# A pad of 48 or 64 floats ahead of the stationary tiles, and when a fourth weight buffer is given up

## The chip, the core and the metric

The kernel runs on one core of a Trainium2 chip. The metric is device time in microseconds, the median of several runs. TensorE (PE) multiplies: it loads a stationary 128 x 128 tile (PEld) and streams a moving one of up to 512 columns past it into PSUM. ScalarE (ACT) and VectorE (DVE) work on tiles in SBUF and PSUM, GpSimd (POOL) mostly issues a few DMAs, and SyncE (SP) issues the DMAs that load the weights. SBUF has 128 partitions; a tile's address is its byte offset within each partition.

## The reference, cut to what matters

Two layers on 256 tokens of width 2048, all in float32. Layer 0 mixes tokens with a convolution module, layer 1 with latent attention of 16 heads. Behind each mixer stands an MLP of width 8192:

```python
for layer in range(DEPTH):
    h = rms_norm(x, norm_mixer_g[layer])
    x = x + (conv_module(h, ...) if layer % 2 == 0 else mla(h, ...))
    h = rms_norm(x, norm_mlp_g[layer])
    x = x + jnp.square(jax.nn.relu(h @ mlp_w1[layer])) @ mlp_w2[layer]
return rms_norm(x, final_norm_g)
```

The MLPs hold most of the arithmetic: x @ w1 (2048 to 8192) and its square's product with w2 (8192 to 2048), twice.

## The kernel before

**Split operands.** A float32 operand is split into an upper part (`hi`, rounded to the matmul's format, made by ScalarE, L465 or L180) and the rest (`lo` = value - `hi`, by VectorE, L466 or L184). A product is then three matmuls, stationary high x moving high, stationary low x moving high, stationary high x moving low (`mm3`, L213 to L215), each with up to 512 columns. Weights arrive by DMA in a `raw` buffer of 1 MB (8 KB in each partition), are split into `hi` and `lo` tiles (six each), and both are moving operands here.

**The MLP.** The hidden width is worked in two halves (`half`, hf = 0 and 1). A half first makes 8 groups g of 512 hidden columns. Each group takes four up units of 1 MB of w1 (`up_products`, L811 and L812; here the weights are stationary and the activations `xt` move), then its four PSUM banks are squared and split into stationary tiles `gh`/`gl`, `mh`/`ml`, `sh`/`sl`, or `dh`/`dl` for the last group (`forms`). Which name a group has depends on how many of its two blocks are worked by Strassen's scheme: none (g = 3 and 6: gh), one (g = 5: mh) or both (g = 0, 1, 2, 4: sh), while g = 7 has a place of its own (dh). Then come two down passes, n = 0 and n = 2, each over 1024 of the 2048 output columns and each of 16 units: 7 plain units (`PlainQuad`, 1 MB of w2, 24 matmuls) and 9 mixed units (`MixedQuad`, Strassen's seven products, 21 matmuls, three DMAs, and sums by VectorE at L516, L520, L521 between its splits). So a half has 32 up units (28 in a first half, whose first group stands ahead) and 32 down units.

**The order.** `run` goes through the list `units` and emits, for each unit i: loads of later units into whatever raw buffers are free (in order of the units), the second split of unit i, the first split of unit i + 1, the further sums and splits of unit i if it is mixed (and then also the second split of a plain unit i + 1, ahead of unit i's last split), the unit's matmuls, and then what hangs in `u.after`. Each engine keeps this order. SP issues loads in this order too, and a load at the head of its queue that waits for its buffer holds back what is behind it.

**The fourth buffer.** There are three raw buffers. At the end of a half's up units the last quarter of `xt` (tag "last", row blocks 12 to 15 of the activations, 8 KB in each partition) is not needed any more, and `open_down` makes it a fourth raw buffer. In a first half it is needed again by the next half's up units: `xt` was copied to DRAM (`save`, L887), and `fetch` (L890) loads it back in pieces of two row blocks. So `retire_raw` gives the fourth buffer up behind unit 11 of pass n = 2, after which no unit is loaded into it, and behind unit 15, the last one, `open_last` makes it the last quarter of `xt` again and `fetch` loads row blocks 12 and 13, 14 and 15. The next half's up units with u = 3 read them. In a second half there is no fetch.

**Places in SBUF.** Pools are stacked from the left: constants, `main` (the residual `xs`), `wpool` (raw, hi, lo), `small`, and behind it the pool of the stage at work: the convolution's, the MLP's (`mp`) or the attention's. A second stack grows from the right: `xt` and what stands in its place (`dh`, `dl` and four `room` tiles beside the fourth raw buffer). Tiles named `pad_...` only take up room. `pad_small`, of `PAD_SMALL` floats in each partition, is the first tile of `small`, so its size moves all tiles of the stages' left pools, and none of wpool or of the right stack.

Of the kernel before, what the change touches and what calls it, by code (L numbers as in the profile page):

```python
# [35 lines left out]
CHUNK = 64  # L36
HALVES = 2
PAD_CONST = 8
PAD_SMALL = 48
PAD_RIGHT = 48  # L40
PAD_KV = 8
PAD_O = 56
# [38 lines left out]
def trunk_kernel(  # L81
# [50 lines left out]
    for i, eps in enumerate((EPS, LN_EPS)):  # L132
        eps_cols[eps] = pad_const[:, i : i + 1]
        nc.vector.memset(eps_cols[eps], eps)
    small.tile([P, PAD_SMALL], F32, tag="pad_small", name="pad_small", bufs=1)
    edge = ctx.enter_context(tc.tile_pool(name="edge", bufs=1, side="right"))
# [238 lines left out]
    def open_rest(name):  # L375
        xt[2] = xt_tile(right_pool(name, 1, 1), KC // 2, "rest")

    def xrows(k, n):
        i, at = ((0, 0), (2, 4), (2, 4), (3, 12))[k // 4]
        return xt[i][:, k - at : k - at + n, :]  # L380
# [174 lines left out]
    class Sums:  # L555
# [19 lines left out]
        def mixed(self, b, fh, fl, end):  # L575

            self.open(True)
            u1, u6, u7, u5 = self.u
            work = [
                (self.e[0][1], 5, b.b22), (u5, 6, b.q1), (u1, 0, b.b11), (self.e[0][0], 1, b.b21),  # L580
                (u6, 3, b.q2), (u7, 4, b.q3), (self.e[1][0], 2, b.q4),
            ]
            for ps, i, (wh, wl) in work:
                mm3(ps, fh[:, i, :], fl[:, i, :], wh, wl, self.first(ps), end and any(ps is u for u in self.u))
# [109 lines left out]
    def mlp(layer, ssq, next_gain, finish=None, before=None, between=None, beside=None, after_up=None):  # L694

        with ExitStack() as cx:
# [16 lines left out]
            ks = [4 * g + 2 * b for g, b in plain]  # L713
            mixed = lambda g: [b for b in range(2) if (g, b) in ms]
            number = [sum(len(mixed(g)) == n for g in range(ng)) for n in range(3)]
            units, rstd = [], []

            def raw_tile():
                return wpool.tile([P, 4 * NB], F32, tag="raw", name=nm("raw"), bufs=3)
# [23 lines left out]
            def run():  # L743


                todo = list(units)
                for i, u in enumerate(units):
                    while todo and any(e not in held for e in free):
                        e, e.place = todo.pop(0), [p for p in free if p not in held][0]
                        free.remove(e.place)  # L750
                        e.load(e.place())
                    if i == 0:
                        u.first()
                        u.main_sum()
                    u.second()
                    for e in units[i - 1].mid if i else ():
                        e()
                    for e in u.at:
                        e()
                    ahead = units[i + 1 : i + 2]  # L760
                    for e in ahead:
                        e.first()
                    u.other_sums()
                    for e in ahead:
                        e.main_sum()
                    u.third()
                    if isinstance(u, MixedQuad):
                        for e in ahead:
                            if not isinstance(e, MixedQuad):
                                e.second()  # L770
                    u.fourth()
                    free.append(u.place)
                    u.products(u)
                    for e in u.after:
                        e()

            def scales():
# [87 lines left out]
            def half(hf):  # L865
# [23 lines left out]
                def fetch(k):  # L889
                    nc.sync.dma_start(xrows(k, 2).bitcast(F32), spare[:, k : k + 2, :])  # L890
# [45 lines left out]
                def mixed_unit(sums, i):  # L936
                    g, b = ms[i]

                    def src():
                        top, low = row_of((sums.n, i))  # L940
                        return top[:, :NB], low, made[sums.n, i]

                    unit(MixedQuad, src, lambda q: sums.mixed(q, *gs[g][b], i == len(ms) - 1))

                def plain_unit(sums, k, at=(), end=False):
                    unit(
                        PlainQuad, rows(w, k_lo + k, 2, sums.n * NB, 2 * NB),
                        lambda q: sums.plain(q.parts, hi, lo, k, end), at,
                    )

                for n in range(0, NNB, 2):
                    sums = Sums(n, (0, 1) if n == 0 else () if last else (1,))
                    final = last and n == NNB - 2
                    order = ks if n == 0 else ks[-2:] + ks[:-2]
                    head = HEAD[n // 2]
                    tail = LAST_TAIL if final and finish is not None else 2 if final else 1
                    inner = len(order) - head - tail
                    m, start = 0, len(units)
                    for i, k in enumerate(order[: len(order) - tail]):
                        plain_unit(sums, k)  # L960
                        if i < head - 1:
                            continue
                        upto = -(-len(ms) * (i - head + 2) // (inner + 1))
                        while m < upto:
                            mixed_unit(sums, m)
                            m += 1
                    if final:
                        for i in range(2):
                            units[-4 + i].after.append(lambda i=i: prepare(i, what="s"))
                        break  # L970
                    plain_unit(sums, order[-1], [lambda sums=sums: sums.join(room)], True)
                    closing.append([lambda sums=sums, n=n: sums.close(down_room if n == 0 else room)])
                    if n:
                        units[start + 4].after.append(lambda: open_rest(f"xt{layer}{hf}"))
                        for i, k in enumerate(range(KC // 4, 3 * KC // 4, 2)):
                            units[start + 5 + 2 * i].after.append(lambda k=k: fetch(k))
                        units[start + 11].after.append(retire_raw)
                        units[start + 15].after.append(open_last)
                        for k in (12, 14):
                            units[start + 15].after.append(lambda k=k: fetch(k))  # L980
                if not last:
                    return

                with tc.manual_schedule():
                    run()
# [27 lines left out]
            for hf in range(HALVES):  # L1013
                nssq = half(hf)
# [4 lines left out]
    with ExitStack() as cx:  # L1019
# [235 lines left out]
        with tc.manual_schedule():  # L1255
# [272 lines left out]
            for m in range(NP):  # L1528
# [4 lines left out]
                for j in range(2):  # L1533
                    k = 2 * m + j
# [19 lines left out]
                for q in {NP - 3: (0, 1, 4), NP - 2: (5, 2, 3), NP - 1: (6, 7)}.get(m, ()):  # L1554
                    t, i = divmod(q, NNB)
# [13 lines left out]
    def rotary_tables():  # L1569
# [60 lines left out]
        nc.scalar.activation(cos, an2, AF.Sin)  # L1630

    ssq = mlp(0, ssq, g_mix[1], beside=rotary_tables)
    repool("a", acc=6, tr=2)


    with ExitStack() as cx:
# [23 lines left out]
        units, pieces = [], {}  # L1660
# [184 lines left out]
        later = []  # L1845
# [112 lines left out]
        with tc.manual_schedule():  # L1958
# [9 lines left out]
            for k in range(KC):  # L1968
                u, j = divmod(k, 2)
# [17 lines left out]
            for k in range(KC):  # L1987
                u, j = divmod(k, 4)
# [105 lines left out]
    with ExitStack():  # L2094
# [60 lines left out]
        def between(ssq, t):  # L2155
# [5 lines left out]
            gained(t, n)  # L2161

        mlp(1, ssq, None, finish, before, between, after_up=load_gf)


# [24 lines left out]
```

## Time and profile before

| What | Value |
|---|---|
| Median of 3 runs (lowest, highest) | 1941.53 us (1941.08, 1941.58) |
| The profiled execution, its own time | 1941.04 us |
| Its span in the profile | 1939.3 us |
| Granted TensorE clock, mean | 0.999 |
| PE, PEld busy | 1920.7 us (99%), 1678.4 us (87%) |
| DVE, ACT, POOL busy | 1541.1 us (79%), 1149.5 us (59%), 315.8 us (16%) |
| Matmuls | 10775 |
| DMA | 428.50 MB, mean 221 GB/s |
| Stages by time, about | convolution 0 to 300 us, MLP of layer 0 to 985, attention to 1245, MLP of layer 1 to the end |

The profile is of one execution. A row of a timeline has the start in us from the span's start, the duration in us, the engine, the line of the kernel, the operation with output and inputs, the count of like instructions merged, and in brackets how long the engine had been idle and what ended that. A row of a grouped view has busy us and mean ns of one behind the bar. "SPq" is the issue of a DMA by SP, not its transfer. Ends of matmuls are modelled, so the pace of PE is better read from the distance of starts.

### The profile page before, as it was taken

The page shows a single profiled execution, that of the slowest core. Times are in us where ns is not written, and L with a number is a line of the kernel's source. Part 1 is how long each engine was busy: PE and PEld are TensorE (multiplying, and loading weights), DVE is VectorE, ACT ScalarE, POOL GpSimd, SP SyncE. Part 2 cuts the span into 40 slices and gives each one's busy share as a digit, 9 for nine tenths or more (in the row PEclk, how much of TensorE's full clock was granted, in tenths as well). Part 3 has the DMA queues.
Part 4 walks back from the last instruction along what each step waited for, and adds up shares of the span by engine and source line. Part 5 has one row for each costly group of instructions (what it writes and reads, how often), then busy time and mean ns, then how long its engine had stood idle before and what let it go on. Part 6 is the DMA issues. An engine that isn't in the chain of part 4 may idle for free.

```text
span 1939.3 us, 29128 instructions
## 1 busy us (share of the span) xinstructions
PE 1920.7 (99%) x10775; PEld 1678.4 (87%) x10775; DVE 1541.1 (79%) x2472; ACT 1149.5 (59%) x1736; POOL 315.8 (16%) x284
## 2 busy tenths in 40 slices
PE   8999999999999999999999999999999999999998
PEld 8999888888888888888899998888888888888886
DVE  7999987767988676798976666866689977668998
ACT  5667755555665555565676565555556655555665
POOL 6999200110010100001001310011100001000010
PEclk9999999999999999999999999999999999999999
DMA  7766456997687998668565445499866979886684
GB/s 229 213 185 186 154 192 209 280 289 228 224 235 240 300 261 244 196 225 235 201 195 153 141 136 191 154 270 286 265 204 212 275 241 296 245 240 199 207 253 148
DMA packets 252590, 428.50 MB, mean 221 GB/s; under 512 B 21144, under 2 KB 96160, under 8 KB 252192
## 3 DMA queue, kind: packets, MB, share of 16 engines
q1 hardware_dynamic: 234992, 394.75, 62.0%
q0 software_dynamic: 16128, 29.37, 9.2%
q10 hardware_dynamic: 1328, 2.52, 0.4%
q8 instruction: 84, 1.38, 0.3%
q14 instruction: 58, 0.48, 0.1%
HBM read 407.72 MB, written 46.14 MB: 234 GB/s over the span
## 4 chain that ended last, share of the span: by engine, by line
PE 96%; DVE 3%; ACT 0%; DMA 0%; issue 0%; ACTq 0%; DVEq 0%
PE acc L811 24%; PE acc L213 15%; PE acc L215 15%; PE acc L214 15%; PE acc L812 13%; PE acc L1084 8%; PE acc L1547 2%; DVE sum L1171 1%; DMA xs<-in_x 0%; PE acc L1826 0%; PE acc L1825 0%; PE acc L1824 0%; PE tr L277 0%; PE acc L1801 0%; PE acc L1802 0%; PE acc L1803 0%
## 5 line engine op out<-in xcount | busy, mean ns | idle before, releaser
L466 DVE TENSOR_TENSOR lo<-raw,hi 128x1024 fp32r<-128x1024 f32 (+1 forms) x542 | 618.3, 1165 | 255.7 <-ACT hi L465 251.9
L811 PE MATMUL acc<-xt,hi 128*128 128x512 f32 x2048 | 710.5, 390 | 0.0
L465 ACT ACTIVATE hi<-raw 128x1024 fp32r<-128x1024 f32 (+1 forms) x542 | 533.8, 1010 | 291.6 <-DMA raw<-in_mlp_w 96.7
L812 PE MATMUL acc<-xt,lo 128*128 128x256 f32 x2048 | 577.5, 282 | 0.0
L811 PEld LDWEIGHTS acc<-xt,hi 128*128 128x128 f32 x2048 | 384.4, 188 | 80.6
L812 PEld LDWEIGHTS acc<-xt,lo 128*128 128x128 f32 x2048 | 387.1, 189 | 0.2
L180 ACT ACTIVATE hi<-raw 128x1024 fp32r<-128x1024 f32 (+2 forms) x210 | 206.3, 1009 | 63.5 <-PE acc L214 45.0
L184 DVE TENSOR_TENSOR lo<-raw,hi 128x1024 fp32r<-128x1024 f32 (+2 forms) x145 | 164.8, 1156 | 63.6 <-ACT hi L180 59.8
L213 PE MATMUL acc<-hi,sh 128*128 128x512 f32 x512 | 201.1, 393 | 0.0
L215 PE MATMUL acc<-lo,sh 128*128 128x512 f32 x512 | 200.1, 391 | 0.8 <-DVE lo L466 0.8
L882 POOL DMA_DIRECT2D q<-in_mlp_w x72 | 59.9, 832 | 764.0 <-DMA q<-in_mlp_w 758.4
L1084 PE MATMUL acc<-xt,hi 128*128 128x256 f32 x1024 | 180.1, 281 | 0.3 <-ACT b L1366 0.2
L214 PE MATMUL acc<-hi,sl 128*128 128x512 f32 x448 | 175.8, 392 | 0.0
L1171 DVE SCALAR_TENSOR_TENSOR sum<-ub,w_dw,sum 128x256 f32<-128x256 f32 x409 | 164.2, 481 | 3.5 <-ACT sum L1141 3.0
L184 POOL TENSOR_TENSOR lo<-raw,hi 128x1024 fp32r<-128x1024 f32 x65 | 155.0, 2407 | 17.5 <-ACT hi L180 17.5
L1084 PEld LDWEIGHTS acc<-xt,hi 128*128 128x128 f32 x1024 | 154.6, 188 | 1.1 <-ACT xt L1350 0.6
L1084 PE MATMUL acc<-xt,lo 128*128 128x256 f32 x512 | 139.2, 279 | 0.0
L823 ACT ACTIVATE v<-acc 128x256 f32<-128x256 f32 x128 | 45.1, 385 | 133.4 <-PE acc L812 133.4
L465 ACT ACTIVATE hi<-xt 128x1024 fp32r<-128x1024 f32 (+1 forms) x88 | 86.2, 979 | 61.0 <-PE acc L214 24.1
L215 PEld LDWEIGHTS acc<-lo,sh 128*128 128x128 f32 x512 | 96.1, 188 | 24.1 <-DVE lo L466 2.6
L213 PEld LDWEIGHTS acc<-hi,sh 128*128 128x128 f32 x512 | 96.2, 188 | 20.9
L605 POOL DMA_DIRECT2D xs<-v x24 | 21.1, 947 | 557.3 <-ACT v L613 378.5
(331 smaller groups left out, 3185.7 us busy)
## 6 DMA issues: line engine op xcount, KB each, us to landing
raw<-in_mlp_w SPq DMA_DIRECT2D x172, 1024.0 KB, 6.8
raw<-in_conv_w_pw SPq DMA_DIRECT2D x62, 512.0 KB, 5.1
raw<-in_mlp_w SPq DMA_DIRECT2D x56, 512.0 KB, 5.9
q<-in_mlp_w SPq DMA_DIRECT2D x72, 256.0 KB, 8.3
q<-in_mlp_w POOLq DMA_DIRECT2D x72, 256.0 KB, 6.6
raw<-in_conv_w_pw SPq DMA_DIRECT2D x16, 1024.0 KB, 5.0
raw<-in_mla_w_o SPq DMA_DIRECT2D x16, 1024.0 KB, 5.3
raw<-q SPq DMA_DIRECT2D x56, 256.0 KB, 6.6
```

What stands on the lines that cost most here:

```text
L180: nc.scalar.activation(hi, raw[:, js, :], AF.Copy)
L184: eng.tensor_tensor(lo, raw, hi.bitcast(F32), op=ALU.subtract)
L213: nc.tensor.matmul(ps, sh, mh, start=start, stop=False)
L214: nc.tensor.matmul(ps, sl, mh, start=False, stop=False)
L215: nc.tensor.matmul(ps, sh, ml, start=False, stop=stop)
L465: nc.scalar.activation(hi, src, AF.Copy)
L466: nc.vector.tensor_tensor(lo, src, hi.bitcast(F32), op=ALU.subtract)
L811: nc.tensor.matmul(ps[b], wh[:, bs], xhl(k), start=k == 0, stop=False)
L812: nc.tensor.matmul(ps[b][:, :S], wl[:, bs], xh(k), start=False, stop=k == KC - 1)
L882: nc.gpsimd.dma_start(made[key], row_of(key)[0][:, :NB], accum_op=ALU.add)
L1084: nc.tensor.matmul(pss[c][b][:, :S], w[i][:, bs], (xh, xl)[j](k), start=k == i + j == 0, stop=end and k == k0 + nk - 1 and (i, j) == terms ...
L1171: nc.vector.scalar_tensor_tensor(out=out, in0=ubs[c][:, w : w + S], scalar=tap(c, w), in1=base, op0=ALU.mult, op1=ALU.add)
```

## The change

It has two parts. `PAD_SMALL` goes from 48 to 64 floats, 64 bytes more in each partition. And behind pass n = 2 of a first half, the fourth raw buffer is given up behind unit 12 instead of unit 11, and it becomes the last quarter of `xt` again, with its two fetches, behind the first unit of the next half (unit 16 counted from the pass's start) instead of behind unit 15. That unit isn't in the list yet when the pass is built, so the work hangs in a table `later`, by the unit's number.

```diff
-PAD_SMALL = 48
+PAD_SMALL = 64
...
-            units, rstd = [], []
+            units, later, rstd = [], {}, []
...
                     u.products(u)
-                    for e in u.after:
+                    for e in u.after + later.get(i, []):
                         e()
...
-                        units[start + 11].after.append(retire_raw)
-                        units[start + 15].after.append(open_last)
-                        for k in (12, 14):
-                            units[start + 15].after.append(lambda k=k: fetch(k))
+                        units[start + 12].after.append(retire_raw)
+                        later[start + 16] = [open_last] + [lambda k=k: fetch(k) for k in (12, 14)]
```

The first part moves tiles, no instruction. Start of each tile's first buffer in bytes, and what is left of it by 256:

| Tile (role) | Before | left by 256 | After | left by 256 |
|---|---|---|---|---|
| sh, sl of the convolution (stationary) | 126400, 142784 | 192 | 126464, 142848 | 0 |
| sh, sl of the MLP (stationary) | 97728, 126400 | 192 | 97792, 126464 | 0 |
| gh, gl (stationary) | 163264, 171456 | 192 | 163328, 171520 | 0 |
| mh, ml (stationary) | 179648, 185280 | 192 | 179712, 185344 | 0 |
| oh, ol of the attention (stationary) | 123584, 139968 | 192 | 123648, 140032 | 0 |
| kvh, kvl, qh, ql (stationary and moving) | 96736 to 109024 | 224 | 96800 to 109088 | 32 |
| dh, dl (stationary) | 196352, 200448 | 0 | the same | 0 |
| xt (moving; stationary ahead of the attention) | 196384 to 220960 | 32 | the same | 32 |
| raw, hi, lo | 21504 to 91136 | 0 | the same | 0 |

All further buffers and all 128-column slices of these tiles lie a multiple of 256 bytes further on.

The second part changes SP's order and the buffers that ScalarE and VectorE read, in both layers alike. SP at the end of layer 0's first half, before: L481 and L504 to L506 are the loads of plain and mixed units, `spare` is `xt`'s copy in DRAM, L879 a copy for a later mixed unit; `raw<-in_mlp_w 128x2x1024` is a plain unit, `128x4x512` an up unit.

```order
L481 DMA raw_6625<-in_mlp_w 128x2x1024
L504 DMA raw_6656<-in_mlp_w 128x1024
L505 DMA raw_6656<-q_698_5416 128x512
L506 DMA raw_6656<-in_mlp_w 128x512
L890 DMA xt_6422<-spare_3781 128x1024
L481 DMA raw_6744<-in_mlp_w 128x2x1024
L481 DMA raw_6775<-in_mlp_w 128x4x512
L481 DMA raw_6820<-in_mlp_w 128x4x512
L890 DMA xt_6863<-spare_3781 128x1024 x2
L481 DMA raw_6866<-in_mlp_w 128x4x512
L879 DMA q_979_6912<-in_mlp_w 128x512
L481 DMA raw_6914<-in_mlp_w 128x4x512
```

And with the change:

```order
L481 DMA raw_6625<-in_mlp_w 128x2x1024
L504 DMA raw_6656<-in_mlp_w 128x1024
L505 DMA raw_6656<-q_698_5416 128x512
L506 DMA raw_6656<-in_mlp_w 128x512
L890 DMA xt_6422<-spare_3781 128x1024
L481 DMA xt_5517<-in_mlp_w 128x2x1024
L481 DMA raw_6745<-in_mlp_w 128x4x512
L481 DMA raw_6776<-in_mlp_w 128x4x512
L481 DMA raw_6821<-in_mlp_w 128x4x512
L879 DMA q_977_6908<-in_mlp_w 128x512
L890 DMA xt_6910<-spare_3781 128x1024 x2
L481 DMA raw_6913<-in_mlp_w 128x4x512
```

The last plain unit (`raw_6744`) now goes into the fourth buffer (`xt_5517`), each of the next three up units goes into the raw buffer that came free one unit earlier, and the two fetches stand behind the third up unit's load and its copy instead of ahead of that load.

ScalarE at the same place, before: the splits of the last mixed unit (`raw_6656`), with those of the last plain unit among them (`raw_6744`).

```order
L465 ACTIVATE hi_6746<-raw_6656 128x1024
L465 ACTIVATE hi_6777<-raw_6656 128x1024
L465 ACTIVATE hi_6781<-raw_6744 128x1024
L465 ACTIVATE hi_6787<-raw_6656 128x512
L465 ACTIVATE hi_6791<-raw_6744 128x1024
L465 ACTIVATE hi_6795<-raw_6656 128x1024
```

And with the change:

```order
L465 ACTIVATE hi_6747<-raw_6656 128x1024
L465 ACTIVATE hi_6778<-raw_6656 128x1024
L465 ACTIVATE hi_6782<-xt_5517 128x1024
L465 ACTIVATE hi_6788<-raw_6656 128x512
L465 ACTIVATE hi_6792<-xt_5517 128x1024
L465 ACTIVATE hi_6796<-raw_6656 128x1024
```

The order stays; the two splits of the plain unit read the fourth buffer. In both orders the mixed unit's last two splits stand behind the plain unit's first one. VectorE's order follows ScalarE's.

## The prediction

> **What bounds the kernel now.** I read the page's busy shares and the chain that ended last, then the waits of PE.
>
> ```profile
> span 1939.3 us, 29128 instructions
> PE 1920.7 (99%) x10775; PEld 1678.4 (87%) x10775; DVE 1541.1 (79%) x2472; ACT 1149.5 (59%) x1736; POOL 315.8 (16%) x284
> PE 96%; DVE 3%; ACT 0%; DMA 0%; issue 0%; ACTq 0%; DVEq 0%
> PE acc L215 <- DVE lo L466: 1.7, 3, 0.8
> ```
>
> TensorE is busy nearly all the time and 96% of the last chain is its matmuls. Behind the start of the program it waits little: for the low halves that VectorE makes (L466) three times, 1.7 us together. So a gain can come from two places: the pace at which one matmul follows the other, and these few waits. The change touches both, the pad the pace and the buffer two of the three waits.
>
> **The pad: which matmuls, and how much each.** A row by line and shape gives the count and the modelled duration of the products of 512 columns, by the stationary tile (the second name behind the arrow).
>
> ```profile
> L213 PE MATMUL acc<-hi,sh 128*128 128x512 f32 x512 | 201.1, 393 | 0.0
> L213 PE MATMUL acc<-hi,gh 128*128 128x512 f32 x252 | 98.9, 392 | 0.0
> L213 PE MATMUL acc<-hi,oh 128*128 128x512 f32 x128 | 50.9, 398 | 0.0
> L213 PE MATMUL acc<-hi,dh 128*128 128x512 f32 x128 | 49.8, 389 | 0.0
> L213 PE MATMUL acc<-hi,mh 128*128 128x512 f32 x120 | 47.1, 393 | 0.0
> L1547 PE MATMUL acc<-hi,sh 128*128 128x512 f32 x64 | 25.3, 395 | 0.3 <-ACT sh L1495 0.3
> L213 PE MATMUL acc<-hi,xt 128*128 128x512 f32 x32 | 12.9, 403 | 0.0
> ```
>
> sh, gh, mh, oh and the convolution's sh start 192 bytes past a multiple of 256, dh at a multiple of 256, xt 32 bytes past one. The three offsets have three durations: 389, 392 to 398, 403 ns. Since ends are modelled, I take the pace from the starts: the first and last matmul of two plain units (48 products, 47 steps), once with gh, once with dh, and a stretch of 108 products with sh, gh and sh (columns of the last three rows: us, PE busy and count, granted clock, DMA share, GB/s).
>
> ```profile
> 478.79 0.40 PE L213 MATMUL acc<-hi,gh 128*128 128x512 f32 x1
> 489.56 0.39 PE L215 MATMUL acc<-lo,gh 128*128 128x512 f32 x1
> ...
> 555.11 0.39 PE L213 MATMUL acc<-hi,dh 128*128 128x512 f32 x1
> 565.76 0.39 PE L215 MATMUL acc<-lo,dh 128*128 128x512 f32 x1
> ...
> 520.12:544.60 24.48, 24.48 (x108) 1.00 0.66 211
> 555.11:565.90 10.79, 10.79 (x49) 1.00 1.01 285
> 642.90:648.30 5.40, 5.40 (x32) 1.00 1.07 278
> ```
>
> gh: 10.77 us / 47 = 229.1 ns a step. dh: 10.65 / 47 = 226.6 ns. The long stretch: 24.48 / 107 = 228.8 ns. The granted clock is 1.00 in both kinds, and the dh stretch has the busier DMA engines, so neither clock nor transfers make dh the quicker one. I take 2.3 ns a matmul (between 228.8 - 226.6 = 2.2 and 229.1 - 226.6 = 2.5). The tiles that the pad moves from 192 to 0: 512 + 252 + 128 + 120 + 64 = 1076 triples of matmuls (each row above is one of the three lines of a triple), 3228 matmuls. 3228 x 2.3 ns = 7.4 us, all on the path, since PE is the chain.
>
> By the Trainium skill, TensorE: Matmul & The Clock Gate, section Back-to-back issue gap, a warm step takes N / 2.4 + 2.5 ns, for 512 columns an estimate of 215.8 ns, with no term for an operand's address. SBUF — State Buffer, section Specifications (TRN2), gives lines of 16 bytes as the grain at which a read pays; 192 and 0 are both whole lines. By these rules the pad would be worth nothing. The trace's 229.1 against 226.6 ns speaks against them, though dh lies in another pool than the others; this is the first rival below.
>
> **What of it is given back.** Where PE is caught by VectorE, a faster PE only waits longer. I looked for the places at which a low half is ready when PE asks for it.
>
> ```profile
> 498.15 1.22 DVE L466 TENSOR_TENSOR lo<-raw,hi 128x1024 fp32r<-128x1024 f32 x1 [0.58 <-ACT hi L465]
> 512.32 2.35 DVE L466 TENSOR_TENSOR lo<-raw,hi 128x1024 fp32r<-128x1024 f32 x2
> ...
> 513.59 0.50 PE L215 MATMUL acc<-lo,sh 128*128 128x512 f32 x1
> 513.93 0.40 PE L213 MATMUL acc<-hi,sh 128*128 128x512 f32 x1
> ...
> 1866.76 0.50 PE L215 MATMUL acc<-lo,sh 128*128 128x512 f32 x1 [0.82 <-DVE lo L466]
> ```
>
> The first of the two splits from 512.32 ends near 513.54 and PE's matmul starts at 513.59, with 0.34 us to the next instead of 0.23: PE has just run into VectorE, which had no gap since 498.15. What PE gains from there on, (513.6 - 498.2) / 0.229 = 67 matmuls x 2.3 ns = 0.15 us, is lost, and somewhat more, 0.2 us, as ScalarE ahead of that split was tied to PE some 25 matmuls earlier. The same unit of the same pass stands four times in the program: 0.8 us. The wait at 1866.76 comes behind a like run of VectorE: 0.2 us. The head of the convolution's second product, whose first 128 matmuls are fed by ScalarE's swish, I estimate at 128 x 2.3 = 0.3 us, and the last 90 matmuls ahead of the addition that ends layer 0's MLP at 0.2 us. Together 1.5 us. The pad is worth 7.4 - 1.5 = 5.9 us; the bounds are 7.4 (nothing lost) and 4.4 (twice as much lost).
>
> **Tiles that the pad moves from 224 to 32.** kvh, kvl, qh and ql: 96 triples as stationary and 128 as moving operand, 672 matmuls of 256 columns.
>
> ```profile
> L213 PE MATMUL acc<-hi,kvh 128*128 128x256 f32 x64 | 18.2, 284 | 0.0
> L213 PE MATMUL acc<-hi,xt 128*128 128x288 f32 x64 | 19.2, 300 | 0.3 <-DVE xs L607 0.3
> ```
>
> 32 columns more take (389 - 284) / 256 x 32 = 13 ns, so at 32 bytes a matmul costs 300 - 13 = 287 ns against 284 at 224. The upper bound is 672 x 3 ns = 2.0 us; below nothing I allow 0.5 us of gain. I take nothing: 224 and 32 lie equally far from a multiple of 256, and the 3 ns are within what the modelled ends differ by among products of one tile.
>
> **The buffer: what waits now.** At the end of layer 0's first half (ScalarE, VectorE, SP's queue, PE; then layer 1's PE):
>
> ```profile
> 624.37 1.06 ACT L465 ACTIVATE hi<-raw 128x1024 fp32r<-128x1024 f32 x1 [0.36 <-PE acc L214]
> 629.91 2.53 ACT L465 ACTIVATE hi<-raw 128x1024 fp32r<-128x1024 f32 x3 [4.48 <-DMA raw<-in_mlp_w]
> ...
> 614.93 1.89 DVE L466 TENSOR_TENSOR lo<-xt,hi 128x512 fp32r<-128x512 f32 x2
> 626.36 1.22 DVE L466 TENSOR_TENSOR lo<-raw,hi 128x1024 fp32r<-128x1024 f32 x1
> 631.00 1.22 DVE L466 TENSOR_TENSOR lo<-raw,hi 128x1024 fp32r<-128x1024 f32 x1 [3.42 <-ACT hi L465]
> ...
> 623.47 12.09 SPq L481 DMA_DIRECT2D raw<-in_mlp_w  x3
> 635.61 0.97 SPq L890 DMA_DIRECT2D xt<-spare  x2
> ...
> 635.56 0.40 PE L214 MATMUL acc<-hi,ml 128*128 128x512 f32 x1
> 636.36 0.50 PE L215 MATMUL acc<-lo,mh 128*128 128x512 f32 x1 [0.40 <-DVE lo L466]
> 636.70 0.40 PE L213 MATMUL acc<-hi,mh 128*128 128x512 f32 x1
> ...
> 1580.22 0.40 PE L214 MATMUL acc<-hi,ml 128*128 128x512 f32 x1
> 1581.05 0.51 PE L215 MATMUL acc<-lo,mh 128*128 128x512 f32 x1 [0.43 <-DVE lo L466]
> 1581.39 0.40 PE L213 MATMUL acc<-hi,mh 128*128 128x512 f32 x1
> ```
>
> The last plain unit's load is issued at 623.47, when a raw buffer comes free, and lands near 629.9. ScalarE has waited 4.48 us for it, VectorE 3.42 us, and queued behind it in their order are the last splits of the mixed unit that PE is working on. PE stands from 635.79 to 636.36: 0.80 - 0.23 = 0.57 us, and the next step takes 0.34 - 0.23 = 0.11 more. Layer 1: 0.60 + 0.11. Together 1.39 us.
>
> With the change that load goes into the fourth buffer, whose last reader ends at 614.93 + 1.89 = 616.8. It is issued there, 6.6 us earlier, and by the same 6.4 us from issue to landing is there at 623.3, ahead of 625.4, when ScalarE gets to it. Both stalls go: 1.4 us gained; the bounds are nothing (the stall reappears one unit on) and 1.4. The loads of the next three units each leave one unit earlier too. The two fetches of xt (12 and 14) leave one load and one copy later, near 637, with the fourth up unit's load behind them:
>
> ```profile
> xt<-spare SPq DMA_DIRECT2D x12, 512.0 KB, 7.2
> 642.31 0.39 SPq L481 DMA_DIRECT2D raw<-in_mlp_w  x1
> ```
>
> They take 7.2 us to land, near 645. PE needs them at the fourth up unit: the first begins near 642.9, and a unit of 32 matmuls takes 5.5 us (the stretch of 5.40 us above), so at 659.4. The load behind them could not leave before 642.31 anyway, as its buffer is full until then, so the fetches, 0.97 us of SP's time, cost nothing. If that cover were gone, the price is theirs, below.
>
> **The sum.** The profiled execution took 1941.04 us, of which the span is 1939.3 us; 1.7 us lie around it and stay. 1941.04 - 5.9 - 1.4 = 1933.7. The median of the runs is 0.5 us above that execution, so 1934.2 us is the forecast, 0.38% below before.
>
> **The rivals.**
> *The pad is worth nothing* (the quick dh is due to its pool, its place among the units or its neighbours; this is the case that the two pages' rules give): only the stalls go, 1941.5 - 1.4 = 1940.1 us. For it: dh is the only group at 0. Against: xt, in the same pool region as dh, is the slowest, and sh, gh, mh and oh, in three stages, share 229 ns as they share the offset. 7%.
> *The stall only moves*: VectorE's order has other work ahead of the mixed unit's last splits, and PE stops a little later for as long. 1941.5 - 5.9 = 1935.6 us. Against: VectorE's 3.42 us of idle time, six times the stall. 8%, within the range.
> *Slower*: the fetches, now behind the third up unit's load, hold SP's queue, so that the fourth up unit's load or xt's last quarter comes late. It decides from a landing past 659.4, 14 us later than worked out; if an up unit's 5.5 us is lost in both layers, 1941.5 - 5.9 + 11.0 = 1946.6 us. Against: that margin of 14 us. 3%.
>
> **How the numbers follow.** The forecast has 82%. Its own range: at best 7.4 + 1.4 + 0.5 = 9.3 us gained, 1932.2; at worst 4.4 + 1.4 - 2.0 = 3.8, 1937.7; not all ends meet, so 1932.6 to 1936.9, which also takes in the moved stall. About 0.2% (3.9 us) is what a measurement of this kernel tells from no change, so faster means below 1937.6. Forecast and moved stall lie there, 90% less a little for the worst ends: faster 0.88, same 0.09 (the pad worth nothing, and those ends), slower 0.03.
>
> **What would show it.** Steps of 226.6 ns in units of gh, sh and mh; durations of 389 ns in the rows of sh, gh, mh, oh; no wait of PE for L466 near 634 and 1575; longer waits near 513 and 1866. Unchanged steps of 229 ns would make the forecast wrong by the pad's 5.9 us; rows of kvh that lengthen, or a wait of L811 for xt in the second half's first group, by what they show.

## The result, and the profile after

The changed kernel takes 1934.91 us (median of 7 runs, 1934.58 to 1935.18) against 1941.58 us before (7 runs, 1941.08 to 1941.65): a ratio of 0.9966, 95% interval 0.9954 to 0.9978, 6.7 us less. The forecast was 1934.2 us.

The profiled execution took 1935.18 us. From its page the span, the busy shares and the chain that ended last:

```profile
span 1933.4 us, 29130 instructions
PE 1915.0 (99%) x10775; PEld 1678.7 (87%) x10775; DVE 1541.8 (80%) x2472; ACT 1149.8 (59%) x1736; POOL 314.9 (16%) x284
PE 88%; DVE 5%; issue 3%; ACT 3%; DMA 1%; POOL 0%; DVEq 0%; SPq 0%; ACTq 0%; POOLq 0%
```

And the rows of PE's waits that count here (us in total, times, longest), the first from before, the others from after:

```profile
PE tr L1928 <- DVE pr L1922: 0.5, 2, 0.3
...
PE tr L1926 <- DVE pr L1920: 1.2, 2, 0.9
PE acc L215 <- DVE lo L466: 1.0, 1, 1.0
```

PE's busy time fell by 5.7 us of the span's 5.9. The waits for L466 went from three (1.7 us) to one (1.0 us): the two ahead of the up units are gone. A wait of the attention for `pr` stands at 1.2 us, where it was 0.5 (the prediction named only the waits for L466 among those behind the start). And the chain leaves PE more often, 88% against 96%: a quicker PE meets the other engines in more places.

The same groups as before the change, by line and shape (busy us, mean ns of one; L1545 was L1547):

```profile
L213 PE MATMUL acc<-hi,sh 128*128 128x512 f32 x512 | 199.4, 389 | 0.0
L213 PE MATMUL acc<-hi,gh 128*128 128x512 f32 x252 | 98.2, 390 | 0.0
L213 PE MATMUL acc<-hi,oh 128*128 128x512 f32 x128 | 50.6, 396 | 0.0
L213 PE MATMUL acc<-hi,dh 128*128 128x512 f32 x128 | 49.8, 389 | 0.0
L213 PE MATMUL acc<-hi,mh 128*128 128x512 f32 x120 | 46.7, 389 | 0.0
L1545 PE MATMUL acc<-hi,sh 128*128 128x512 f32 x64 | 25.0, 391 | 0.2 <-ACT sh L1493 0.2
L213 PE MATMUL acc<-hi,kvh 128*128 128x256 f32 x64 | 18.3, 287 | 0.0
```

sh, gh and mh now have dh's duration (392 or 393 became 389 or 390), dh itself stands. oh came down to 396 only, not to the 389 that the prediction named as a sign. The starts say the same: the plain unit with gh, first and last of its 48 products,

```profile
478.50 0.39 PE L213 MATMUL acc<-hi,gh 128*128 128x512 f32 x1
489.17 0.39 PE L215 MATMUL acc<-lo,gh 128*128 128x512 f32 x1
```

10.67 us / 47 = 227.0 ns a step, where it was 229.1. Over the whole trace I took the mean distance of starts of successive products of one kind, steps behind which PE had waited left out (more than 40 ns over the median). This is the "step" of all that follows:

| Products of 512 columns, by stationary tile | Before, ns | After, ns |
|---|---|---|
| sh of the MLP | 229.0 | 226.8 |
| gh | 229.0 | 226.9 |
| mh | 229.0 | 226.7 |
| sh of the convolution | 229.1 | 227.2 |
| oh | 229.2 | 227.9 |
| dh (not moved) | 227.1 | 226.8 |
| xt ahead of the attention (not moved) | 233.2 | 233.5 |

Where the time went is read from the starts of the same products in both traces. Negative is gained; the middle column is what the prediction's terms give for the stretch (2.3 ns for each moved product, less the losses it named, and 0.68 or 0.71 us for a stall).

| Stretch (us in before's trace) | Forecast, us | Measured, us |
|---|---|---|
| start to the convolution's second product (0 to 209) | 0 | +0.34 |
| rest of the convolution (to 305) | -0.58 | -0.64 |
| layer 0, first half (to 643) | -1.89 | -1.77 |
| layer 0, second half (to 985) | -1.01 | -1.07 |
| attention (to 1250) | -0.88 | +0.04 |
| layer 1, first half (to 1588) | -1.92 | -1.80 |
| layer 1, second half (to the end) | -1.01 | -0.94 |
| sum | -7.29 | -5.84 |

So in one pair of executions the MLP's four halves and the convolution paid nearly to plan, and the attention and the start did not. (The medians differ by 6.7 us; the pair of profiled executions by 5.9, as the one of before was quick among its kind and the one of after slow.)

The buffer at the end of layer 0's first half (SP's queue, ScalarE, PE):

```profile
615.80 0.38 SPq L481 DMA_DIRECT2D xt<-in_mlp_w  x1
...
624.12 1.04 ACT L465 ACTIVATE hi<-xt 128x1024 fp32r<-128x1024 f32 x1
...
634.24 0.39 PE L214 MATMUL acc<-hi,ml 128*128 128x512 f32 x1
634.47 0.39 PE L215 MATMUL acc<-lo,mh 128*128 128x512 f32 x1
634.70 0.39 PE L213 MATMUL acc<-hi,mh 128*128 128x512 f32 x1
```

The last plain unit's load leaves at 615.80 instead of 623.47, ScalarE comes to it at 624.12 without any idle time, and PE's products follow at 0.23 us each, where it had stood for 0.57 us.

And the place at which PE had just run into VectorE, with its like at the end of layer 1 (VectorE, then PE):

```profile
497.73 1.23 DVE L466 TENSOR_TENSOR lo<-raw,hi 128x1024 fp32r<-128x1024 f32 x1 [0.56 <-ACT hi L465]
500.74 1.29 DVE L847 TENSOR_TENSOR dl<-v,dh 128x512 fp32r<-128x512 f32 x2
511.91 2.35 DVE L466 TENSOR_TENSOR lo<-raw,hi 128x1024 fp32r<-128x1024 f32 x2
...
512.74 0.39 PE L214 MATMUL acc<-hi,sl 128*128 128x512 f32 x1
513.18 0.50 PE L215 MATMUL acc<-lo,sh 128*128 128x512 f32 x1
513.51 0.39 PE L213 MATMUL acc<-hi,sh 128*128 128x512 f32 x1
...
1861.42 0.50 PE L215 MATMUL acc<-lo,sh 128*128 128x512 f32 x1 [0.96 <-DVE lo L466]
```

From 512.74 to 513.18 PE takes 0.44 us for a step of 0.23: 0.21 us of waiting that was not there before, and then the same slow step of 0.33 as before. This is the loss that the prediction put at 0.2 us at each of four places; the one near 1861 grew from 0.99 to 1.12 us by the starts (forecast 0.2 more, measured 0.13).

### The profile page after: what moved, and what is told of

Same layout as the page of the kernel before. It is cut to its first block, busy times and chain, and to the rows that moved or that the text cites. A ratio compares the mean times of both kernels' runs of the same rounds, so it can differ in the third digit from the quotient of the medians.

```text
span 1933.4 us, 29130 instructions
## 1 busy us (share of the span) xinstructions
PE 1915.0 (99%) x10775; PEld 1678.7 (87%) x10775; DVE 1541.8 (80%) x2472; ACT 1149.8 (59%) x1736; POOL 314.9 (16%) x284
## 4 chain that ended last, share of the span: by engine, by line
PE 88%; DVE 5%; issue 3%; ACT 3%; DMA 1%; POOL 0%; DVEq 0%; SPq 0%; ACTq 0%; POOLq 0%
PE acc L811 24%; PE acc L812 13%; PE acc L215 13%; PE acc L213 13%; PE acc L214 13%; PE acc L1082 8%; PE acc L1545 2%; DVE lo L466 1%; DVE sum L1169 1%; ACT hi L465 1%; ACT hi L180 1%; DMA xs<-in_x 0%; DVE lo L184 0%; DMA raw<-in_mla_w_in 0%; PE acc L1935 0%
## 5 line engine op out<-in xcount | busy, mean ns | idle before, releaser
L466 DVE TENSOR_TENSOR lo<-raw,hi 128x1024 fp32r<-128x1024 f32 (+1 forms) x538 | 614.0, 1165 | 248.5 <-ACT hi L465 245.8
L811 PE MATMUL acc<-xt,hi 128*128 128x512 f32 x2048 | 710.5, 390 | 0.0
L812 PE MATMUL acc<-xt,lo 128*128 128x256 f32 x2048 | 577.5, 282 | 0.0
L811 PEld LDWEIGHTS acc<-xt,hi 128*128 128x128 f32 x2048 | 384.4, 188 | 80.6
L812 PEld LDWEIGHTS acc<-xt,lo 128*128 128x128 f32 x2048 | 387.1, 189 | 0.2
L1082 PE MATMUL acc<-xt,hi 128*128 128x256 f32 x1024 | 180.2, 281 | 0.3 <-ACT b L1364 0.2
L1082 PEld LDWEIGHTS acc<-xt,hi 128*128 128x128 f32 x1024 | 154.5, 188 | 1.1 <-ACT xt L1348 0.6
L1082 PE MATMUL acc<-xt,lo 128*128 128x256 f32 x512 | 139.2, 279 | 0.0
L465 ACT ACTIVATE hi<-xt 128x1024 fp32r<-128x1024 f32 (+1 forms) x92 | 90.3, 981 | 63.5 <-DVE xt L521 23.9
L466 DVE TENSOR_TENSOR lo<-xt,hi 128x1024 fp32r<-128x1024 f32 (+1 forms) x92 | 103.6, 1127 | 12.4 <-ACT hi L465 12.2
```

Source lines behind the costliest of these rows:

```text
L465: nc.scalar.activation(hi, src, AF.Copy)
L466: nc.vector.tensor_tensor(lo, src, hi.bitcast(F32), op=ALU.subtract)
L811: nc.tensor.matmul(ps[b], wh[:, bs], xhl(k), start=k == 0, stop=False)
L812: nc.tensor.matmul(ps[b][:, :S], wl[:, bs], xh(k), start=False, stop=k == KC - 1)
L1082: nc.tensor.matmul(pss[c][b][:, :S], w[i][:, bs], (xh, xl)[j](k), start=k == i + j == 0, stop=end and k == k0 + nk - 1 and (i, j) == terms ...
```

## Experiments

### Each part alone

Two kernels, each with one part of the change. The pad alone:

```diff
-PAD_SMALL = 48
+PAD_SMALL = 64
```

> The kernel before with the pad of 64 floats alone; the fourth buffer is given up where it was. Theory (the pace follows the tiles' start, the two stalls have a cause of their own): steps of 226.7 ns in the units of sh, gh, mh, oh; PE still stands near 634 and 1577 us, by 0.7 us each or a little more, since the faster PE arrives there earlier; 1936.3 us, 1.4 us above the changed kernel. Rival (all of the gain is the pad's, and the stalls were hidden in it): 1934.9 us, as the changed kernel.

Measured: 1936.52 us against 1941.52, ratio 0.9975 (0.9965 to 0.9985), 5.0 us gained. The steps are those of the changed kernel (226.8 ns); the stall ahead of the up units stays:

```profile
633.70 0.39 PE L214 MATMUL acc<-hi,ml 128*128 128x512 f32 x1
634.74 0.50 PE L215 MATMUL acc<-lo,mh 128*128 128x512 f32 x1 [0.65 <-DVE lo L466]
```

From start to start 1.04 us for a step of 0.23, 0.81 us of stall, 0.24 more than before, as the quicker PE comes earlier and the load does not.

The buffer alone is the changed kernel with the old pad:

```diff
-PAD_SMALL = 64
+PAD_SMALL = 48
```

> The changed kernel with the pad back at 48 floats, so that the later giving up of the fourth buffer is left alone. Theory: both stalls for L466 at the ends of the first halves are gone, steps stay at 229 ns, 1941.5 - 1.4 = 1940.1 us. Rival (the stall only moves to another unit): 1941.5 us and a wait of about 0.6 us elsewhere in the same passes.

Measured: 1940.27 us against 1941.52, ratio 0.9994 (0.9984 to 1.0003), 1.25 us gained. Near 634 PE keeps its step:

```profile
634.22 0.39 PE L214 MATMUL acc<-hi,ml 128*128 128x512 f32 x1
634.46 0.39 PE L215 MATMUL acc<-lo,mh 128*128 128x512 f32 x1
```

No wait for L466 has come in the stalls' place, and by the groups gh is as slow as before:

```profile
L213 PE MATMUL acc<-hi,gh 128*128 128x512 f32 x252 | 98.9, 393 | 0.0
```

The interval takes in 1, though each of the ten runs (1939.98 to 1940.84) lies below each of the 17 of before (1941.00 and more). The trace, in which both stalls are gone, shows where the time went. The parts nearly add up: 5.0 + 1.25 = 6.25 us against 6.7 together; that layer 0's stall grows by 0.24 us under the pad alone is some of the difference. The rival of the pad worth nothing and that of the stall only moving both fall here.

### Other remainders by 256

If the remainder is what counts, which remainders are quick? Three kernels differ from the changed one in `PAD_SMALL` alone.

```diff
-PAD_SMALL = 64
+PAD_SMALL = 80    (sh, gh, mh, oh at 64; 72 gives 32, 96 gives 128)
```

> The changed kernel with a pad of 80 floats: the stationary tiles start 64 bytes past a multiple of 256 instead of 0 (kvh and qh 96). Theory (what counts is the largest power of two that divides the start, 64 for 64 as for 192): steps of 229.0 ns as before the change, 1940.1 us as with the buffer alone. Rival (what counts is the remainder itself, from 6.7 ns at 32 falling to 2.3 ns at 192, so 5.8 ns at 64): steps of 232.5 ns, 3228 x 5.8 = 18.7 us less what is given back, 1950 to 1953 us.

> The changed kernel with a pad of 72 floats: the stationary tiles start 32 bytes past a multiple of 256 (kvh and qh 64), as xt does in both kernels. Theory and the remainder's rival alike: steps of 233.3 ns, as the products with xt as stationary tile have them, 3228 x 6.6 = 21 us less what PE's waits for VectorE swallow, 1951 to 1956 us. Rival (xt's 233 ns are due to its place or to its neighbours, not to its start): steps of 226.7 or 229 ns, 1935 to 1940 us.

Measured: with 64 left 1953.88 us (ratio to before 1.0063, 1.0046 to 1.0079), with 32 left 1952.77 us (1.0057, 1.0042 to 1.0072). Both are slower than before the change, by 11 to 12 us. The unit with gh at 64:

```profile
480.58 0.39 PE L213 MATMUL acc<-hi,gh 128*128 128x512 f32 x1
491.54 0.39 PE L215 MATMUL acc<-lo,gh 128*128 128x512 f32 x1
```

10.96 / 47 = 233.2 ns. At 32 it is 233.3, just the step of xt, which lies at 32. My theory, that the largest power of two in the offset counts, so that 64 would be as good as 192, was wrong; the rival's 232.5 ns at 64 was near. The xt products are slow by their start, not by being xt.

> As the changed kernel, but the pad puts sh, gh, mh and oh 128 bytes past a multiple of 256 (kvh and qh 160 past one). The theory left by the runs at 0, 32, 64 and 192: the start of a stationary tile sets the step by its remainder, 226.7 ns at 0, 229.0 at 192, 233.3 at 32 and 64. If the cost falls evenly from 64 to 192, 128 gives some 231 ns and about 1947 us. Rival one, a second threshold lies between 128 and 192: 233.3 ns and 1953 us as at 32 and 64. Rival two, it lies between 64 and 128: 229 ns and 1940.3 us as at 192. The first rule that I had, that the largest power of two in the offset counts, would give less than 229 ns; it has failed at 64 already.

Measured: 1950.64 us, ratio 1.0049 (1.0035 to 1.0063), steps of 232.4 ns in sh, gh, mh and oh. 128 is nearly as bad as 64; the cost does not fall evenly towards 192.

### Is it the start, or the pool?

In the prediction the first rival took dh to be quick for its pool or its neighbours. The pad ahead of dh and dl was made 64 bytes longer, which puts them at 192:

```diff
-PAD_DOWN = 8
+PAD_DOWN = 24
```

> As the changed kernel, but the pad ahead of dh and dl is 64 bytes longer, so that they, in the other pool, start 192 bytes past a multiple of 256 and all else stays. The theory, that the start alone counts: dh's 384 products go from 226.7 to 229.0 ns a step, 0.9 us, 1935.8 us, no other step moves. The rival, that the pool or the neighbours made dh quick: dh stays at 226.7 ns, 1934.9 us.

Measured: 1935.73 us (0.9972, 0.9960 to 0.9983), expected 1935.8. dh alone got slower:

```profile
L213 PE MATMUL acc<-hi,gh 128*128 128x512 f32 x252 | 98.2, 390 | 0.0
L213 PE MATMUL acc<-hi,dh 128*128 128x512 f32 x128 | 50.3, 393 | 0.0
```

dh's step went from 226.8 to 229.5 ns, nothing else moved, and by the starts of the same products the trace falls 0.9 us behind, 0.12 to 0.17 at each of dh's stretches. The start decides, in this pool too.

### All tiles at multiples of 256

If 0 is best for a tile, all should lie there. Four more pads were changed:

```diff
-PAD_RIGHT = 48
-PAD_KV = 8
-PAD_O = 56
-PAD_DOWN = 8
+PAD_RIGHT = 56
+PAD_KV = 64
+PAD_O = 64
+PAD_DOWN = 64
```

> As the changed kernel, with four more pads changed, so that xt and the attention's tiles (kvh, qh, kpA, kT, qpA, pT, vv) start at multiples of 256 bytes instead of 32 past one; sh, gh, mh, oh and dh stay at 0. If only the stationary operand's start counts: xt as stationary operand 233.4 to 226.7 ns in 96 products of 512 columns (0.6 us), the 288 of kvh, kvl, qh, ql perhaps 1 to 2 ns (0.3 us); L811, which moves xt past stationary hi, stays at 228.4 ns; about 1934.0 us. The rival, that the moving operand's start counts as well: L811 goes from 228.4 to 226.7 ns, 2048 times, 3.5 us more, about 1930.6 us.

Measured: 1953.93 us, ratio 1.0064 (1.0051 to 1.0077), 19 us slower than the changed kernel. Neither theory had that. L811 and L812 and the xt products, all with xt:

```profile
L811 PE MATMUL acc<-xt,hi 128*128 128x512 f32 x2048 | 724.0, 399 | 0.0
L812 PE MATMUL acc<-xt,lo 128*128 128x256 f32 x2048 | 575.2, 281 | 0.0
L213 PE MATMUL acc<-hi,xt 128*128 128x512 f32 x32 | 12.7, 398 | 0.0
```

As stationary operand xt did gain from 0 (404 ns became 398; the step 233.5 became 228.6). As moving operand it lost: L811's step went from 228.4 to 236.2 ns, 2048 x 7.8 = 16.0 us, and the convolution's 1536 products of 256 columns (L1082) from 116.8 to 119.9 ns, 4.8 us. L812 alone went the other way, from 118.3 to 117.1 ns, 2.5 us. So a moving operand's start counts as well, and 0 is not a good start by itself.

### Start, or distance?

That left two readings: each operand has good and bad starts of its own, or the distance between the two operands counts. One kernel moves every tile by 64 bytes, so that no distance modulo 256 changes but every start does:

```diff
-PAD_CONST = 8
-PAD_RIGHT = 48
+PAD_CONST = 24
+PAD_RIGHT = 32
```

> As the changed kernel, but the first pad of the left side is 64 bytes longer and the first of the right side 64 bytes shorter, so that every tile, moving and stationary alike, starts 64 bytes further past a multiple of 256 (hi, lo, raw, sh, gh, mh, oh and dh at 64, xt and kvh at 96), and all distances modulo 256 stay as they are. The theory now, after xt at 0 made L811 slower: what counts is where the stationary tile starts against the moving one, modulo 256; the steps stay at 226.7 ns and L811 at 228.4 ns, 1934.9 us. The rival, that each operand's own start counts: sh, gh, mh and oh go to 233.3 ns as at 64 before, about 1953 us, and dh too.

Measured: 1937.40 us, ratio 0.9977 (0.9968 to 0.9986). That is 2.5 us more than the changed kernel, and not the 18 us of the rival. The steps are the same in every kind: sh 226.8, gh 226.9, mh 226.7, dh 226.7, oh 227.9, xt 233.5, L811 228.4.

```profile
L811 PE MATMUL acc<-xt,hi 128*128 128x512 f32 x2048 | 710.5, 390 | 0.0
L213 PE MATMUL acc<-hi,sh 128*128 128x512 f32 x512 | 199.4, 389 | 0.0
L213 PE MATMUL acc<-hi,gh 128*128 128x512 f32 x252 | 98.1, 389 | 0.0
```

Among PE's waits a new one stands:

```profile
PE sum L312 <- DMA stage<-in_mla_kv_norm_g: 1.6, 1, 1.6
```

The 2.5 us lie at the start: by the starts of the same products this trace is 2.15 us behind at 64 us and 2.27 us at the end, and this wait of 1.6 us, for a small load of the norms' vectors near 27 us, makes most of it. In 1860 us of products nothing differs by more than 0.15 us in all. With sh, gh, mh and oh at 64 and hi at 0 the step was 233.3 ns; with all of them at 64 it is 226.8. It is the place of one operand against the other that counts. (Whole distances stayed the same here, so that 256 is the period rests on other runs: sh, gh and mh, at different distances with one remainder, have one step in each kernel. What else moved along, such as the tiles that ScalarE and VectorE write meanwhile, is not told apart by this run; the run with xt moved shows that it is enough to move the moving operand.)

Two more distances were tried, both with the later subtraction of the next section, against whose 1933.47 us they are to be held.

```diff
-PAD_RIGHT = 48
-PAD_DOWN = 8
+PAD_RIGHT = 40
+PAD_DOWN = 16
```

> The changed kernel with the later subtraction for dl (1933.5 us), and with xt 64 bytes past a multiple of 256 instead of 32 (dh stays at 0). L811 took 228.4 ns with xt at 32 and 236.2 ns with xt at 0. If the cost falls with the distance from 0, 64 gives less than 228.4 ns, at best 226.7 as sh: 1933.5 - 3.5 = 1930.0 us. The rival: 32 is near the best and 64 lies beyond it, L811 over 230 ns, 1937 us or more. L812 and the attention's small tiles, moved too, may add or take 1 us.

Measured: 1943.44 us, ratio 1.0008 (0.9999 to 1.0017), 10 us more. L811 took 231.7 ns on average, but not evenly: 233.8 and 232.9 ns in the two first halves, 230.0 and 230.1 in the second ones, though xt starts at the same remainder in all. With xt at 32 all four halves have 228.4. Layer 1's first half itself has two paces: its first five up units take 229.8 to 230.4 ns a step, all later ones 232.9 to 234.1. The change stands behind two small products that break the stream:

```profile
1275.31 0.38 PE L783 MATMUL acc<-ident,y 128*128 128x128 f32 x2
```

The places of xt and of the weights' tiles are the same on both sides of it. A first copy of xt to DRAM (L887) leaves there too, but layer 0's first half is at the slow pace from its first unit on, ahead of its first copy near 330 us. So at this distance a stream can run at either of two paces, and the remainder by 256 does not settle which; what does is open.

```diff
-PAD_SMALL = 64
-PAD_KV = 8
-PAD_O = 56
+PAD_SMALL = 56
+PAD_KV = 24
+PAD_O = 40
```

> The changed kernel with the later subtraction for dl (1933.5 us), and with sh, gh, mh and oh 224 bytes past a multiple of 256, so that the moving hi starts 32 bytes further on than they do; kvh and qh at 64; dh stays at 0. If the step is even in the distance (226.7 ns at 0, 229.0 at 64), 32 gives some 227.9 ns and 3228 x 1.2 = 3.9 us more: 1937 us. The rival: 32 bytes is the best distance for these products too, as it is of the three that L811 was given (236.2 at 0, 228.4 at 32, 231.7 at 64): below 226.7 ns, 1932 us or less. kvh and qh at 64 give back 0.9 us in both.

Measured: 1952.68 us, ratio 1.0058 (1.0045 to 1.0070). Both expectations missed: 233.3 ns in sh, gh, mh and oh, the worst step again, between two better ones. dh, left at 0, stayed at 227.2. The products with hi or lo as moving operand, then, over all runs:

| Stationary tile past a multiple of 256 (hi, lo at 0) | 0 | 32 | 64 | 128 | 192 | 224 |
|---|---|---|---|---|---|---|
| step, 512 columns, ns | 226.7 | 233.3 | 233.3 | 232.4 | 229.0 | 233.3 |

The row is for gh and mh and for sh in the MLP. At 0 the convolution's sh (227.2), oh (227.9) and xt (228.6) have a higher mean; the section on the prediction shows why.

### VectorE's run ahead of the wait

The loss at 512.74 comes at the end of a run in which VectorE has hardly a gap from 497.73 on. One row in it, L847, is not for the products at hand: it makes dl, whose first unit begins at 544, more than 40 us later. Its two instructions take 1.29 us together. Its due time was moved:

```diff
-LAST_TICKS = (4, 5, 8, 11, 13, 15)
+LAST_TICKS = (4, 5, 8, 11, 13, 24)
```

> As the changed kernel, but the last due time of the table LAST_TICKS is 24 instead of 15: VectorE's subtraction for dl (L847, 1.29 us, twice) comes later in the next half's work. The theory, that the pad's missing 0.9 us went into the four places where PE catches up with VectorE (0.21 + 0.11 us at 512.74 and the three like it): with the subtraction out of the way these waits of 0.32 us each go, 1.3 us, about 1933.6 us. The rival, that VectorE is only as late somewhere else, or that dl now comes late for PE: the waits stand elsewhere, 1934.9 us or more.

Measured: 1933.47 us, ratio to before 0.9959 (0.9947 to 0.9972), 1.44 us under the changed kernel. The time alone would not carry so small a difference, but the trace shows it at its place (VectorE, PE):

```profile
510.60 2.35 DVE L466 TENSOR_TENSOR lo<-raw,hi 128x1024 fp32r<-128x1024 f32 x2
512.87 1.29 DVE L847 TENSOR_TENSOR dl<-v,dh 128x512 fp32r<-128x512 f32 x2
...
512.20 0.39 PE L213 MATMUL acc<-hi,sh 128*128 128x512 f32 x1
512.42 0.39 PE L214 MATMUL acc<-hi,sl 128*128 128x512 f32 x1
512.65 0.39 PE L215 MATMUL acc<-lo,sh 128*128 128x512 f32 x1
```

L847 now stands behind the two splits, the splits come 1.3 us earlier (0.3 of it is a lead from the program's start), and PE keeps its step. Against the changed kernel's trace the starts jump ahead by 0.36, 0.35, 0.38 and 0.34 us at the four places, 1.43 us together, and lose it nowhere. dl comes in time.

### A version that beats both

At 64 bytes kvh, kvl, qh and ql had the quickest steps of all as stationary operand (115.2 and 114.4 ns with the other tiles at 32). With the later subtraction:

```diff
-PAD_KV = 8
-PAD_O = 56
+PAD_KV = 16
+PAD_O = 48
```

> The changed kernel with the later subtraction for dl (1933.5 us), and kvh, kvl, qh and ql 64 bytes past a multiple of 256 instead of 32; all else stays. At 64 their 288 products as stationary operand took 115.2 and 114.4 ns a step against 118.2 (with sh at 32): 288 x 3.3 = 0.9 us, 1932.6 us. The rival, that these small steps hide behind the weight loads or that the attention waits for other engines there: 1933.5 us.

Measured: 1932.77 us against 1941.37 before, ratio 0.9960 (0.9946 to 0.9974), the lowest median of all kernels, 2.1 us under the changed one. Two of its five runs took 1934.6 and 1934.7 us, so the 0.7 us against the later subtraction alone rests on the trace more than on the times. The steps are 114.6 and 114.1 ns, and against the kernel with the later subtraction alone the starts gain 0.6 us between 1007 and 1168 us, in the attention, where these tiles are.

## Why the prediction was right, and where not

**The bound.** PE's pace was the bound, as read from the chain: 5.7 of 5.9 us of the span came out of PE's busy time.

**The pad's 2.3 ns.** Right in size (229.0 to 226.7 or 226.8 in MLP and 229.1 to 227.2 in the convolution) and in the places. For oh it was mis-sized: 1.3 ns, 0.5 us instead of 0.88. The trace shows where oh's steps are longer. The heads' small products (L1926, L1935 and others) break oh's stream into 13 stretches. Behind such a break the first ten steps take 229.8 ns on average (118 steps; 229.4 before the change), the others 226.7 (240 steps; 228.9 before). Ten steps behind a break, then ten of the last stretch, by their first and last start:

```profile
1150.93 0.39 PE L214 MATMUL acc<-hi,ol 128*128 128x512 f32 x1
1153.23 0.40 PE L215 MATMUL acc<-lo,oh 128*128 128x512 f32 x1
...
1226.07 0.39 PE L215 MATMUL acc<-lo,oh 128*128 128x512 f32 x1
1228.33 0.39 PE L213 MATMUL acc<-hi,oh 128*128 128x512 f32 x1
```

These are 2.30 us against 2.26. With xt at 0 its products have the same two paces, 230.6 and 226.7 ns. The convolution's sh takes 228.8 ns up to 228 us, where it still waits now and then, and 226.7 from there to the end of its first 192 products. So 226.7 ns is the pace to which these streams settle, and right behind such a break the pad gained nothing. Why it takes some ten products to settle is open.

**The cause behind it** was named too simply. "Multiples of 256" stood for a property of the tile; the runs show a relation between the stationary and the moving tile, which in the MLP's and the attention's products comes to the same, as hi and lo lie at 0. A kernel made by that reading, all tiles at 0, was 19 us slower.

**Given back, 1.5 us.** The four places like 513.59 cost 0.21 us, as worked out (0.2), and the cause, VectorE's gapless run, is shown by the run that moved L847 out of it. In the first halves there is a further small loss of 0.05 near 574. The rows of the convolution and of the MLP's halves agree with the table to 0.12 us, in part because errors cancel. At the convolution's head the first 64 products gained 0.02 us and the next 64 gained 0.14, so about 0.15 us was lost there and not 0.3; and of the 0.2 us put down for the last 90 matmuls of layer 0's MLP nothing shows, as the starts gain 0.15 us from 965 to 980 us, the full pace. Against that, the step gained 2.2 ns in the MLP and 1.9 in the convolution, not 2.3.

**kvh, kvl, qh, ql at nothing.** Right as a sum: as stationary operand 117.0 to 118.2 ns (288 x 1.2 = 0.35 us lost), as moving operand 118.3 to 116.9 (384 x 1.4 = 0.5 us gained). The reason given, that 224 and 32 are equally far from a multiple of 256, was wrong: 64 is 3.6 ns quicker than 32, and 0 is slower (119.8).

**The buffer's 1.4 us.** Right: 0.69 and 0.70 us in the trace, 1.25 us as a part alone. The load left 7.7 us earlier, of which 1.1 us is PE's lead by then; the fetches moved behind cost nothing, as no wait of L811 shows. The rival of the held queue fell with it.

**The rival that the pad is worth nothing** fell: 2.3 to 6.6 ns a step hang on where the tiles start. The formula that the prediction drew on stands in the Trainium skill, TensorE: Matmul & The Clock Gate, section Back-to-back issue gap, for a single matmul by itself; for a stream that section gives about 131 ns at 512 columns, and no step of 512 columns here was near it. The Trainium skill, TensorE: Matmul & The Clock Gate, section Step-by-step: what each phase is for, says besides that TensorE reads moving operand and weights through two independent ports, so that loading the next weights takes nothing from the running product. By that no distance between the two could matter; the runs with everything moved by 64 bytes and with xt moved, taken together, speak against it. That the two reads get in each other's way is an inference from this, not something a trace shows.

**The sum** came out 0.7 us too low against the median and 1.5 us against its own profiled execution. The larger misses, beside oh's 0.4 us, are two terms that it did not have. One is 0.34 us by 209 us, nearly all of it a jump of 0.32 at 13.9 us; the traces of other kernels jump against that of the changed one by about 0.4 us near there too, either way. The other is the attention's wait for `pr`, 0.40 us by the starts before and 1.11 after. VectorE and GpSimd, before and after:

```profile
1071.78 1.22 DVE L184 TENSOR_TENSOR lo<-raw,hi 128x1024 fp32r<-128x1024 f32 x1 [2.20 <-ACT hi L180]
1071.78 1.55 POOL L1648 TENSOR_TENSOR m<-scratch,cos 128x128 f32<-128x128 f32 x1
```

```profile
1068.67 1.54 DVE L184 TENSOR_TENSOR lo<-raw,hi 128x1024 fp32r<-128x1024 f32 x1 [2.20 <-ACT hi L180]
1068.67 0.46 POOL L1646 TENSOR_TENSOR m<-scratch,cos 128x128 f32<-128x128 f32 x1
1069.09 1.44 POOL L1647 TENSOR_TENSOR m<-scratch,sin 128x128 f32<-128x128 f32 x1
```

In both, an instruction of each engine starts at the same time. Before, VectorE's took 1.22 us and GpSimd's was stretched to 1.55; after, GpSimd's went through in 0.46 and VectorE's took 1.54. VectorE is 0.3 us later there, and again 0.3 us at its next split (1.22 for 0.95 us), and PE waits for what stands behind. The buffer alone, the pad alone and every other kernel run here had 0.59 to 1.30 us at this place; only the profiled execution of before had 0.40. So neither part is shown to be its cause, and with one trace of before it can't be told whether 0.40 is usual there.

## What to carry to other kernels

Where TensorE is the bound, compare the distance of starts among like matmuls that differ only in where their tiles lie: here 226.7 to 233.3 ns for the same product, which made 1% of the whole time. Leave out the first products behind a break in the stream, or look at them by themselves. Then move one operand against the other and measure, since no rule of "align it" held: of the starts tried 0 was best for one pair of tiles and worst for another, and a step of 32 bytes either way can cost more than the last change gained. And when PE gets faster, look at the places where another engine is busy without a gap ahead of it; work there that isn't due yet can be moved behind.

## What the runs showed of the hardware

- A sequence of 512-column fp32 products at a granted clock of 1.00 took 226.7 to 233.3 ns a step by the place of the stationary tile against the moving one modulo 256 bytes (table above), and not in an even course: 224 gave 233.3 between 229.0 at 192 and 226.7 at 0.
- Moving all tiles by 64 bytes left the step of each 512-column kind as it was to 0.1 ns.
- Behind a break by smaller products, oh's stream at 0 took 229.8 ns a step for its first ten and 226.7 from then on; xt's, with xt at 0, took 230.6 and 226.7.
- With a product of 512 and one of 256 columns in turn (L811, L812) the good distance was another: 236.2 ns with xt at 0, 228.4 at 32, and at 64 either about 230 or about 233 to 234, with a switch between the two in mid-stream at 1275 us.
- For 256 columns with kvh and kvl stationary: 119.7 ns at 0, 118.2 at 32, 114.6 at 64, 117.8 at 96, 119.9 at 160, 117.1 at 224.
